# Splitting memory pools so that the next stage's first steps may be issued among the last steps of the stage before

## The chip, the cores and the metric

The kernel runs on one core of one Trainium2 chip. The metric is the device time of one execution in microseconds (us), median of several runs. All numbers of the trace come from one profiled execution of the kernel before.

## The reference, cut to what matters

One layer of a hybrid encoder over a prompt of 2048 frames with 16 meta tokens in front, and over 64 further frames of a running stream. All is in float32.

```python
h = rms_norm(x, attn_norm); z = h @ w_in          # one projection, its columns split into
q_lat, kv_lat, k_rope, qkv, gate, beta, a = split(z)
# group A: latent attention, 8 heads, chunk-causal (chunks of 64 frames)
q = rope(rms_norm(rms_norm(q_lat) @ w_uq)); k = rope(rms_norm([kv_lat @ w_uk, k_rope])); v = kv_lat @ w_uv
attn = softmax(mask(q @ k.T * 96**-0.5)) @ v
# group B: gated delta rule, 4 heads of 128, after a causal convolution of width 4 and SiLU
q, k, v = l2(silu(conv(qkv)));  S_t = decay_t * S_(t-1) + beta_t * k_t (v_t - k_t S)   # in exact chunked form
gdn = rms_norm(q_t S_t) * silu(gate)
x = x + [rms_norm(attn), gdn] @ w_out;  y = x + relu(rms_norm(x) @ w_up)**2 @ w_down
```

The chunked form of the delta rule needs, for each chunk of frames and each head, the inverse of a triangular matrix (independent of other chunks), and then one step of a recurrence in the state S (each chunk after the one before).

## The kernel before

A float32 product is made of three matmuls: each operand is split into a high part and the rest (`split`: a copy on ScalarE and a subtraction on VectorE), and high x high, high x low, low x high are summed in PSUM. [...]

**The program's order.** The kernel is written with pools of named tiles. A pool lies on one of two stacks (left and right), and a tile waits for the users of earlier tiles on its own bytes or its own bank. A scheduler puts the instructions of each engine in one fixed order when the program is built: of the instructions that it holds to be ready it takes the one with the best rank, and the rank is the place in the program. `high_priority(n)` lets the instructions traced inside it rank n places earlier.

**Phase A (`phase_a`), the projection.** The 2128 frames form five blocks (`BLOCKS`: 336, 512, 512, 512 and 256 frames). `load_x` keeps each block's input, split, as `hhi`, `hlo`, all five in one pool `h` (136 KB a partition). The 22 columns of weights (128 wide each) are walked in the order of `BATCHES`; for each batch the blocks are walked, and for each block and column `col_product` makes one product of 24 matmuls (L270 to L272) into a bank `ps` (six banks of the pool `aps`; two more, `psn`, hold sums of squares). `col_finish` multiplies it by `rstd` on VectorE (L282), which frees the bank. Columns 18, 19 and 20, the last, are three of the four columns of the output gate; each is a batch of its own, so the blocks are walked three times. Their SiLU takes three steps on ScalarE (L369 to L371) and one on VectorE (L372), and goes to `gateT` in memory. `load_w` brings a column's weights through two buffers `wraw` (L256), scales them on VectorE (L258) and splits them (L134, L135).

**Phase G (`phase_g`), the delta rule.** It goes by rounds. In each round every open generator takes one step: the preparations of chunks (`gdn_prep`, at most `GK` = 4 at once, a new one when the round and the counts `GR`, `GF`, `GL0`, `GA` allow it), the recurrence of one chunk (`gdn_scan`), and, from round `QS` on, `q_gen` (the queries, 17 tiles, in a pool on the right stack) and after it the attention's first keys and the first part of `prep` of its first job. A preparation loads `kv` and `kq` (L446, L448), turns k (L455), makes squares, an inverse root (`rsqrt`: two steps on ScalarE, L141 and L142, four on GpSimd, L143 to L146) and the normalised keys `kn` (L485, VectorE), turns these (L489), and goes on to the triangular inverse, in banks `gpp` (5 banks). A scan makes the new values (L598, L599), the new state `S` (L605, L607) and the output `o` (L619, L627), squares it, makes an inverse root over ScalarE and GpSimd, scales `o` on GpSimd (L638) and turns it (L642), in banks `gps` (2 banks). All tiles lie in one pool `g`, all seven banks in one pool.

**Attention (`attention`).** 32 jobs (a pair of heads, one of the two, a block of 512 queries). `prep` of a job turns the queries into `qh`, `ql` (L935), makes the scores' row maxima in banks `pspre` (L964 matmul, L965 maximum on VectorE), turns them (L970) and writes their negative into a row of `qh` by a transfer (L972, L973). `main_block` makes the scores `pss` (L994 to L996), the exponent `P` (L998), its split, and the sum over the values `pso` (L1011 to L1013). Both stand in one pool of PSUM banks, `b_ps`; some tags of SBUF tiles have a part of their buffers in a pool that opens early (`EARLY`), during phase G.

Of the kernel before, what the change touches and what calls it, by code (L numbers as in the profile page):

```python
# [40 lines left out]
RUNS = [(0, 1), (1, NS), (NS, NS + 1), (NS + 1, 18)]  # L41
BATCHES = [[21, 3, 4]] + [[5 + i] for i in range(12)] + [[17], [0, 1, 2], [18], [19], [20]]
WRB, APB, ZTB, XTB = 2, 6, 6, 4
# [3 lines left out]
GB = {"kq": 4, "qk": 5, "kd": 5, "vn": 5, "uf": 5, "wt": 5, "ss": 5, "kv": 2, "sq": 1, "kn": 1, "lg": 1, "dm": 2, "db": 1, "bn": 1,  # L47
      "kneg": 3, "bh": 4, "bl": 4, "tt": 5, "uu": 5, "q16": 2, "rk": 3, "se": 1, "vw": 2, "S": 3, "o1": 1, "o": 1, "fr": 2}
GR, GK, GA, GF, GL0 = 6, 4, 5, 2, 4
QSB, QS = 2, 5  # L50
EARLY = {"lath0": 1, "latl0": 1, "kr0": 1, "ssr0": 1, "V0": 2, "KTh0": 2, "KTl0": 2, "raw": 1, "rt": 1,
         "wkv_h": 1, "wkv_l": 1, "qn": 1, "qh": 1, "ql": 1, "kn": 1, "ksq": 2, "kss": 2, "krk": 2, "ktmp": 2}
QP = 2
# [65 lines left out]
class Prog:  # L119
# [42 lines left out]
    def phase_a(self):  # L162
        nc, I = self.nc, self.I
        with ExitStack() as es:
# [21 lines left out]
            for n, batch in enumerate(BATCHES):  # L186
                nxt = BATCHES[n + 1] if n + 1 < len(BATCHES) else []
                Wn = [self.load_w(ct) for ct in nxt[:3 - len(batch)]]
                for b in range(len(BLOCKS)):
                    zs = []  # L190
                    for ct, w in zip(batch, W):
                        ps = self.col_product(w, b)
# [19 lines left out]
    def load_x(self, b):  # L212
# [3 lines left out]
        n = b1 - b0  # L216
        hi = self.hp.tile([128, 8, n], F32R, name=f"hhi{b}")
        lo = self.hp.tile([128, 8, n], F32R, name=f"hlo{b}")
        self.h.append((hi, lo))
# [17 lines left out]
    def mean_rstd(self, ss, n, w, r=None):  # L237

        nc = self.nc
        ps = self.aps.tile([128, NB], F32, name="ps_n", tag="psn", bufs=2)  # L240
        nc.tensor.matmul(ps[:, :n], self.ones, ss, start=True, stop=True)
# [19 lines left out]

    def col_product(self, w, b):

# [168 lines left out]
    def gt(self, tag, bufs=1, shape=(128, 4, 128), dt=F32):  # L432
        return self.gp.tile(list(shape), dt, name=tag, tag=tag, bufs=GB.get(tag, 1))

    def gpsum(self, kind="p"):
        return self.gps.tile([128, 4, 128], F32, name="gp" + kind, tag="gp" + kind, bufs=GPS[kind])

# [210 lines left out]
    def phase_g(self, g=True, q=True, eb=None):  # L648

        with ExitStack() as es:  # L650
            eq = es.enter_context(ExitStack())
            qp = self.pool(eq, "q", side="right")
            qps = self.pool(eq, "q_ps", space=PSUM, side="right")
            self.gp = self.pool(es, "g")
            self.gps = self.pool(es, "gps", space=PSUM)
            self.state = None
            self.lev = [[self.gp.tile([128, 4, 128], F16, name=f"lev{j}{i}") for i in range(7)] for j in range(NL)]
            qg = self.q_gen(qp, qps) if q else iter(())
            ek = None
            for _ in range(QP):  # L660
                next(qg, None)
            Ps = [{"first": i < NL} for i in range(len(CHUNKS))]
            preps, scan, started, scanned, rounds = [], None, 0, 0, 0
            began = [-GL0] * NL
            while g and scanned < len(CHUNKS):

                if rounds >= max((started - GF) * GR, began[started % NL] + GL0) and len(preps) < GK and started < min(len(CHUNKS), scanned + GA):
                    preps.append(self.gdn_prep(CHUNKS[started], Ps[started]))
                    began[started % NL] = rounds
                    started += 1  # L670
                rounds += 1
                if rounds > QS:
                    if ek is not None:
                        if next(ek, "x") == "x" and self.first_prep is None:
                            self.first_prep = self.prep((0, 0, 0))
                            next(self.first_prep)
                    elif next(qg, "x") == "x" and eb is not None:
                        eq.close()
                        self.attn_early(eb)
                        ek = self.early_keys = self.keys(0, 0)  # L680
                if scan is None and "uf" in Ps[scanned]:
                    scan = self.gdn_scan(CHUNKS[scanned], Ps[scanned])
                if scan is not None and next(scan, "x") == "x":
                    scan, scanned = None, scanned + 1
                for p in list(preps):
                    if next(p, "x") == "x":
                        preps.remove(p)
            for _ in qg:
                pass
# [107 lines left out]
    def bpsum(self, tag):  # L797
        k = self.count.get("ps" + tag, 0)
        self.count["ps" + tag] = k + 1
        early = tag == "m" and (self.bp is None or k % BPS["m"] == 0)  # L800
        pool, n = (self.eps_, 1) if early else (self.bps, BPS[tag] - (tag == "m"))
        return pool.tile([128, 512], F32, name="ps" + tag, tag=tag, bufs=n)
# [231 lines left out]
    def attention(self):  # L1034
        with ExitStack() as es:
# [57 lines left out]

            while prep and prep[0][2] == 0:
                prep_step()
            for n, job in enumerate(jobs):
# [834 lines left out]
```

## Time and profile before

| | us |
|---|---|
| median of 3 runs (lowest, highest) | 3327.87 (3316.88, 3330.03) |
| the profiled execution | 3322.66 |
| its span | 3320.9 |
| TensorE busy | 3196.8 (96%) |
| VectorE busy | 2650.8 (80%) |
| ScalarE busy | 1558.4 (47%) |
| GpSimd busy | 400.5 (12%) |

The span is the time from the first to the last instruction of the profile. PE is TensorE's matmuls, DVE VectorE, ACT ScalarE, POOL GpSimd, SP SyncE, whose queue issues most transfers. PEclk is the clock that was granted to TensorE, as a share of full speed. Busy times of one engine do not overlap, those of different engines do.

### The profile page before, as it was taken

How to read it: one execution, taken by the hardware profiler on the slowest of the kernel's cores; microseconds unless marked ns; L12 is line 12 of the kernel's file. 1: busy time of each engine (PE TensorE's matmuls, PEld its weight loads, DVE VectorE, ACT ScalarE, POOL GpSimd, SP SyncE). 2: the span in 40 equal slices, each digit the busy share in tenths (PEclk: the TensorE clock that was granted, in tenths of full speed). 3: DMA queues.
4: the chain of work that ended last, by engine and by line, in shares of the span. 5: the costliest groups of instructions: out<-in, count | busy, mean ns of one | idle time of the engine just before them, and what ended most of it. 6: DMA issues, size and time to landing. Idle time of an engine off the chain costs nothing.

```text
span 3320.9 us, 54512 instructions
## 1 busy us (share of the span) xinstructions
PE 3196.8 (96%) x20037; PEld 2943.1 (89%) x20037; DVE 2650.8 (80%) x5438; ACT 1558.4 (47%) x3495; POOL 400.5 (12%) x758
## 2 busy tenths in 40 slices
PE   9999998998979999999899999999999999999999
PEld 6888887888867778887799999999999999999999
DVE  8877654788758788888789888888888888988887
ACT  5555524555536868787564222334333333422232
POOL 0100013675510000000201000011000002100000
PEclk9999998999978999999999999999999999999999
DMA  4322213233221011010332222233222225122222
GB/s 132 91 74 70 74 63 100 87 104 100 59 57 35 20 34 34 25 37 26 106 99 75 77 77 75 76 110 109 88 76 73 65 73 160 58 73 77 77 74 70
DMA packets 318091, 248.09 MB, mean 75 GB/s; under 512 B 31776, under 2 KB 291616, under 8 KB 317760
## 3 DMA queue, kind: packets, MB, share of 16 engines
q1 hardware_dynamic: 300256, 219.21, 22.8%
q10 hardware_dynamic: 15536, 16.23, 1.6%
q0 software_dynamic: 2032, 9.18, 0.8%
q8 instruction: 157, 2.57, 0.3%
q14 instruction: 110, 0.90, 0.1%
HBM read 196.99 MB, written 47.52 MB: 74 GB/s over the span
## 4 chain that ended last, share of the span: by engine, by line
PE 83%; DVE 8%; ACT 2%; DMA 2%; issue 2%; POOL 1%; SPq 0%; POOLq 0%; DVEq 0%; ACTq 0%
PE psu L1601 23%; PE psd L1601 21%; PE ps L270 5%; PE ps L271 5%; PE ps L272 5%; PE pss L994 2%; PE pso L1011 2%; PE pss L995 2%; PE pss L996 2%; PE pso L1013 2%; PE pso L1012 2%; PE pspre L964 2%; DVE hl L1581 0%; PE psm L889 0%; DMA qh<-mrow 0%
## 5 line engine op out<-in xcount | busy, mean ns | idle before, releaser
L1601 PE MATMUL psu<-hh,uh 128*128 128x352 f32 x1728 | 563.0, 326 | 2.6 <-ACT uh L1497 2.1
L1601 PE MATMUL psu<-hl,uh 128*128 128x352 f32 x1728 | 557.3, 323 | 0.0
L1601 PE MATMUL psu<-hh,ul 128*128 128x352 f32 x1728 | 549.9, 323 | 0.0
L1601 PE MATMUL psd<-al,dh 128*128 128x352 f32 x1536 | 496.0, 323 | 3.5 <-DVE al L1790 3.2
L1601 PE MATMUL psd<-ah,dl 128*128 128x352 f32 x1536 | 494.6, 322 | 0.0
L1601 PE MATMUL psd<-ah,dh 128*128 128x352 f32 x1536 | 473.3, 324 | 11.1 <-DVE y L1709 7.4
L1709 DVE TENSOR_TENSOR y<-y,psd 128x352 f32<-128x352 f32 x768 | 386.6, 515 | 103.5 <-PE psd L1601 101.5
L1601 PEld LDWEIGHTS psu<-hh,uh 128*128 128x128 f32 x1728 | 325.7, 189 | 4.5 <-ACT uh L1497 2.5
L1601 PEld LDWEIGHTS psu<-hl,uh 128*128 128x128 f32 x1728 | 326.1, 189 | 1.2 <-issue 0.5
L1601 PEld LDWEIGHTS psu<-hh,ul 128*128 128x128 f32 x1728 | 323.9, 188 | 0.2 <-DVE ul L1475 0.2
L270 PE MATMUL ps<-hhi,whi 128*128 128x512 f32 (+5 forms) x880 | 313.6, 360 | 9.7 <-ACT hhi L134 7.1
L272 PE MATMUL ps<-hhi,wlo 128*128 128x512 f32 (+5 forms) x880 | 314.0, 358 | 0.0
L271 PE MATMUL ps<-hlo,whi 128*128 128x512 f32 (+5 forms) x880 | 312.5, 356 | 0.3 <-DVE hlo L135 0.2
L1601 PEld LDWEIGHTS psd<-ah,dh 128*128 128x128 f32 x1536 | 284.1, 188 | 16.9 <-DVE y L1709 11.5
L1601 PEld LDWEIGHTS psd<-al,dh 128*128 128x128 f32 x1536 | 289.1, 188 | 5.5 <-DVE al L1790 5.4
L1497 ACT CAST dh<-wr 128x512 fp32r<-128x512 f32 x192 | 119.3, 621 | 367.2 <-PE psd L1601 324.8
L1601 PEld LDWEIGHTS psd<-ah,dl 128*128 128x128 f32 x1536 | 288.8, 188 | 0.0
L1788 ACT CAST ah<-u 128x352 fp32r<-128x352 f32 x192 | 93.4, 487 | 398.6 <-DVE u L1786 280.0
L135 DVE TENSOR_TENSOR Pl<-P,Ph 128x512 fp32r<-128x512 f32 (+4 forms) x352 | 211.2, 611 | 52.2 <-ACT Ph L134 49.7
L998 ACT ACTIVATE P<-pss 128x512 f32<-128x512 f32 (+4 forms) x352 | 185.9, 539 | 87.6 <-PE pss L996 76.9
L965 DVE TENSOR_REDUCE mp<-pspre 128x1 f32<-128x296 f32 (+6 forms) x400 | 189.1, 500 | 31.1 <-PE pspre L964 29.2
L1714 POOL TENSOR_TENSOR y<-y,v 128x352 f32<-128x352 f32 x40 | 40.8, 1043 | 1330.8 <-DVE y L1709 1330.7
(458 smaller groups left out, 7266.5 us busy)
## 6 DMA issues: line engine op xcount, KB each, us to landing
wr<-in_w_up SPq DMA_DIRECT2D x192, 256.0 KB
wr<-in_w_down SPq DMA_DIRECT2D x192, 256.0 KB
qn<-scr_qN SPq DMA_DIRECT2D x32, 384.0 KB
wr<-in_w_out SPq DMA_DIRECT2D x48, 256.0 KB
wraw<-in_w_in SPq DMA_DIRECT2D x42, 256.0 KB
scr_convT<-s SPq DMA_DIRECT2D x36, 256.0 KB
mixr<-scr_mixT SPq DMA_DIRECT2D x12, 704.0 KB
out_y_T<-y SPq DMA_DIRECT2D x48, 176.0 KB
```

The source lines that it names most:

```text
L135: (lo_eng or nc.vector).tensor_tensor(lo, src, hi.bitcast(F32), op=ALU.subtract)
L270: nc.tensor.matmul(ps[:m, :n], whi[:, k, :m], hi[:, k], start=k == 0, stop=False)
L271: nc.tensor.matmul(ps[:m, :n], whi[:, k, :m], lo[:, k], start=False, stop=False)
L272: nc.tensor.matmul(ps[:m, :n], wlo[:, k, :m], hi[:, k], start=False, stop=k == 7)
L964: nc.tensor.matmul(ps[:, :z - a], qh[:r, i * 128:(i + 1) * 128], kh[:r, a:z], start=True, stop=True)
L965: nc.vector.tensor_reduce(m[:, i:i + 1] if one else mp[:, j:j + 1], ps[:, :z - a], axis=AX.X, op=ALU.max)
L994: nc.tensor.matmul(ps[:w, off:], kh[:r, s:s + w], qh[:r, off:], start=True, stop=False)
L998: nc.scalar.activation(p[:w, off:], ps[:w, off:], AF.Exp)
L1497: self.nc.scalar.copy(t[0], src)
L1601: self.nc.tensor.matmul(ps, w, h, start=i == 0, stop=i == len(steps) - 1)
L1709: adds.append(nc.vector.tensor_tensor(Y[j][:, d], Y[j][:, d], ps, op=ALU.add).ins)
L1788: done = nc.scalar.copy(A[f, j][0], u).ins
```

## The change

The projection's columns 18, 19 and 20 become one batch. Each block's `h` gets a pool of its own. The two banks `psn` get a pool of their own on the right side (`apn`); the pool `aps` with the six banks is closed before the last batch, and the last batch's products take the two `psn` banks. In phase G a new pool `g_early` is opened below `g`; of each tag's buffers a part (`EG`) lies there and the rest in `g`, in the same rotation. The banks `p` and `s` get a pool each. The first two steps of the queries and the first `HR` = 12 rounds rank `HO` = 360 places earlier. In the attention, `m`, `mp` and `mrow` get a buffer in the early pool, the banks are divided into two pools (`pre` and `s`, `o` and `m`), and the steps of the first job's `prep` before the first main block rank `AO` = 150 places earlier.

```diff
-BATCHES = [[21, 3, 4]] + [[5 + i] for i in range(12)] + [[17], [0, 1, 2], [18], [19], [20]]
+BATCHES = [[21, 3, 4]] + [[5 + i] for i in range(12)] + [[17], [0, 1, 2], [18, 19, 20]]
...
+EG = {"kv": 2, "kq": 3, "lg": 1, "ss": 3, "sq": 1, "dm": 2, "db": 1, "rk": 3, "vn": 3, "kn": 1, "bn": 1, "qk": 3, "kd": 2, "kneg": 2,
+      "bh": 3, "bl": 3, "tt": 3, "uu": 3, "q16": 1, "uf": 1}
...
+HR, HO = 12, 360
+AO = 150
...
-         "wkv_h": 1, "wkv_l": 1, "qn": 1, "qh": 1, "ql": 1, "kn": 1, "ksq": 2, "kss": 2, "krk": 2, "ktmp": 2}
+         "wkv_h": 1, "wkv_l": 1, "qn": 1, "qh": 1, "ql": 1, "kn": 1, "ksq": 2, "m": 1, "mp": 3, "mrow": 1, "kss": 2, "krk": 2, "ktmp": 2}
...
-            self.hp = self.pool(es, "h")
+            self.hp = [self.pool(es, f"h{b}") for b in range(len(BLOCKS))]
...
-            self.aps = self.pool(es, "aps", space=PSUM)
+            self.apn = self.pool(es, "apn", space=PSUM, side="right")
+            ea = es.enter_context(ExitStack())
+            self.aps = self.pool(ea, "aps", space=PSUM)
...
+                if not nxt:
+                    ea.close()
...
-        ps = self.aps.tile([128, NB], F32, name="ps", tag="ps", bufs=APB)
+        if last:
+            ps = self.apn.tile([128, NB], F32, name="ps", tag="psn", bufs=2)
+        else:
+            ps = self.aps.tile([128, NB], F32, name="ps", tag="ps", bufs=APB)
...
     def gt(self, tag, bufs=1, shape=(128, 4, 128), dt=F32):
-        return self.gp.tile(list(shape), dt, name=tag, tag=tag, bufs=GB.get(tag, 1))
+        k, n, e = self.gcount.get(tag, 0), GB.get(tag, 1), EG.get(tag, 0)
+        self.gcount[tag] = k + 1
+        early = k % n < e
+        return (self.ge if early else self.gp).tile(list(shape), dt, name=tag, tag=tag, bufs=e if early else n - e)
...
+            self.ge, self.gcount = self.pool(es, "g_early"), {}
             self.gp = self.pool(es, "g")
-            self.gps = self.pool(es, "gps", space=PSUM)
+            self.gps = {k: self.pool(es, "gp" + k, space=PSUM) for k in "ps"}
...
-            for _ in range(QP):
-                next(qg, None)
+            with self.tc.high_priority(HO):
+                for _ in range(QP):
+                    next(qg, None)
...
+                with ExitStack() as early:
+                    if rounds < HR:
+                        early.enter_context(self.tc.high_priority(HO))
...
-        self.bps = self.pool(es, "b_ps", space=PSUM)
+
+        a, b = (self.pool(es, "b_ps" + k, space=PSUM) for k in "ab")
+        self.bps = {"pre": a, "s": a, "o": b, "m": b}
...
-            while prep and prep[0][2] == 0:
-                prep_step()
+            with self.tc.high_priority(AO):
+                while prep and prep[0][2] == 0:
+                    prep_step()
```

The body of a round is unchanged inside the new `with`.

## Rows read from the trace of the kernel before

**Rows 1.** The page: busy time and instructions of each engine; granted clock in 40 slices.

```profile
PE 3196.8 (96%) x20037; PEld 2943.1 (89%) x20037; DVE 2650.8 (80%) x5438; ACT 1558.4 (47%) x3495; POOL 400.5 (12%) x758
...
PEclk9999998999978999999999999999999999999999
```

**Rows 2.** Busy time by stretch: length, PE, PEld, DVE, ACT, POOL busy (instructions), clock, DMA.

```profile
540.00:550.00 10.00, 2.05 (x16) 1.59 (x14) 7.28 (x18) 5.13 (x26) 6.41 (x15) 0.82 0.79 247
550.00:560.00 10.00, 9.19 (x45) 8.12 (x45) 6.94 (x13) 4.04 (x8) 6.62 (x6) 0.50 0.43 112
560.00:600.00 40.00, 35.33 (x294) 29.50 (x293) 25.65 (x57) 20.14 (x71) 25.86 (x49) 0.83 0.24 67
600.00:700.00 100.00, 94.95 (x884) 84.07 (x883) 80.09 (x161) 55.18 (x192) 67.04 (x138) 0.98 0.34 98
945.00:985.00 40.00, 28.00 (x107) 22.47 (x108) 23.77 (x72) 15.73 (x46) 5.88 (x16) 0.59 0.26 73
```

**Rows 3.** Timeline of PE around the first seam: start, length, instruction [idle before, releaser].

```profile
468.76 0.32 PE L270 MATMUL ps<-hhi,whi 128*128 128x336 f32 x1
...
515.88 0.32 PE L270 MATMUL ps<-hhi,whi 128*128 128x336 f32 x1
...
519.58 0.40 PE L270 MATMUL ps<-hhi,whi 128*128 128x512 f32 x1
...
538.81 0.60 PE L455 MATMUL gpp<-ident,kv 128*16 128x128 f32 x4
...
550.46 0.57 PE L489 MATMUL gpp<-ident,kn 16*128 16x16 f32 x4 [8.11 <-DVE kn L485]
...
559.91 0.44 PE L728 MATMUL qp<-wuq_h,ql_h 128*128 128x384 f32 x1
```

**Rows 4.** Timeline of SP's queue around the first seam.

```profile
519.62 0.37 SPq L446 DMA_DIRECT2D kv<-scr_convT  x1
...
541.87 0.82 SPq L700 DMA_DIRECT2D qs<-in_w_uq  x2
```

**Rows 5.** Timeline of PE up to the attention's first scores.

```profile
814.46 0.62 PE L935 MATMUL psm<-ident,qn 128*96 128x128 f32 x4
...
936.03 1.12 PE L642 MATMUL gps<-ident,o 128*128 128x128 f32 x4 [5.07 <-POOL o L638]
936.94 0.64 PE L598 MATMUL gps<-vn,uf 128*128 128x128 f32 x2
...
948.87 1.12 PE L642 MATMUL gps<-ident,o 128*128 128x128 f32 x4 [5.12 <-POOL o L638]
949.64 1.12 PE L964 MATMUL pspre<-KTh,qh 105*128 105x144 f32 x3
951.04 0.94 PE L964 MATMUL pspre<-KTh,qh 96*128 96x264 f32 x2 [0.28 <-DVE m L965]
...
958.43 0.58 PE L889 MATMUL psm<-wkv_h,lath 128*128 128x256 f32 x1 [0.41 <-ACT mrow L972]
...
961.15 0.63 PE L994 MATMUL pss<-qh,KTh 97*80 97x512 f32 x1
```

**Rows 6.** Timeline of DVE around the first seam.

```profile
530.70 0.69 DVE L282 TENSOR_TENSOR zt<-ps,rstd 128x512 f32<-128x512 f32 x1 [1.94 <-PE ps L272]
...
536.14 0.69 DVE L282 TENSOR_TENSOR zt<-ps,rstd 128x512 f32<-128x512 f32 x1 [1.94 <-PE ps L272]
539.01 0.42 DVE L282 TENSOR_TENSOR zt<-ps,rstd 128x256 f32<-128x256 f32 x1 [2.18 <-PE ps L272]
...
549.64 0.68 DVE L485 TENSOR_TENSOR kn<-gpp,rk 16x512 f32<-16x512 f32 x1 [2.66 <-POOL rk L146]
```

**Rows 7.** Timeline of DVE: the weights loaded for the last column.

```profile
477.01 1.34 DVE L258 TENSOR_TENSOR wraw<-wraw,g_attn 128x512 f32<-128x512 f32 x2 [2.59 <-DMA wraw<-in_w_in]
...
478.87 0.69 DVE L135 TENSOR_TENSOR wlo<-wraw,whi 128x512 fp32r<-128x512 f32 x1
```

**Rows 8.** Timeline of DVE: the state that the last chunk reads.

```profile
928.32 0.69 DVE L607 TENSOR_TENSOR S<-se,gps 128x512 f32<-128x512 f32 x1 [0.66 <-PE gps L605]
```

More of the change, by code (lines that the diff above doesn't have):

```diff
@@ L191, in phase_a @@
                     for ct, w in zip(batch, W):
-                        ps = self.col_product(w, b)
+                        ps = self.col_product(w, b, n + 1 == len(BATCHES))
                         new = n == 0 and ct == batch[0]
@@ L216, in load_x @@
         n = b1 - b0
-        hi = self.hp.tile([128, 8, n], F32R, name=f"hhi{b}")
-        lo = self.hp.tile([128, 8, n], F32R, name=f"hlo{b}")
+        hi = self.hp[b].tile([128, 8, n], F32R, name=f"hhi{b}")
+        lo = self.hp[b].tile([128, 8, n], F32R, name=f"hlo{b}")
         self.h.append((hi, lo))
@@ L239, in mean_rstd @@
         nc = self.nc
-        ps = self.aps.tile([128, NB], F32, name="ps_n", tag="psn", bufs=2)
+        ps = self.apn.tile([128, NB], F32, name="ps_n", tag="psn", bufs=2)
         nc.tensor.matmul(ps[:, :n], self.ones, ss, start=True, stop=True)
@@ L260, in load_w, with col_product @@
         return hi, lo, m
-    def col_product(self, w, b):
+    def col_product(self, w, b, last=False):
         nc = self.nc
@@ L432, in gt @@
     def gt(self, tag, bufs=1, shape=(128, 4, 128), dt=F32):
-        return self.gp.tile(list(shape), dt, name=tag, tag=tag, bufs=GB.get(tag, 1))
+        k, n, e = self.gcount.get(tag, 0), GB.get(tag, 1), EG.get(tag, 0)
+        self.gcount[tag] = k + 1
+        early = k % n < e
+        return (self.ge if early else self.gp).tile(list(shape), dt, name=tag, tag=tag, bufs=e if early else n - e)
     def gpsum(self, kind="p"):
-        return self.gps.tile([128, 4, 128], F32, name="gp" + kind, tag="gp" + kind, bufs=GPS[kind])
+        return self.gps[kind].tile([128, 4, 128], F32, name="gp" + kind, tag="gp" + kind, bufs=GPS[kind])
     def gdn_prep(self, n, P):
@@ L653, in phase_g @@
             qps = self.pool(eq, "q_ps", space=PSUM, side="right")
+            self.ge, self.gcount = self.pool(es, "g_early"), {}
             self.gp = self.pool(es, "g")
-            self.gps = self.pool(es, "gps", space=PSUM)
+            self.gps = {k: self.pool(es, "gp" + k, space=PSUM) for k in "ps"}
             self.state = None
-            self.lev = [[self.gp.tile([128, 4, 128], F16, name=f"lev{j}{i}") for i in range(7)] for j in range(NL)]
+            self.lev = [[self.ge.tile([128, 4, 128], F16, name=f"lev{j}{i}") for i in range(7)] for j in range(NL)]
             qg = self.q_gen(qp, qps) if q else iter(())
             ek = None
-            for _ in range(QP):
-                next(qg, None)
+            with self.tc.high_priority(HO):
+                for _ in range(QP):
+                    next(qg, None)
             Ps = [{"first": i < NL} for i in range(len(CHUNKS))]
@@ L665, in phase_g @@
             while g and scanned < len(CHUNKS):
[L667 to L687, printed above, removed]
+                with ExitStack() as early:
+                    if rounds < HR:
+                        early.enter_context(self.tc.high_priority(HO))
+                    if rounds >= max((started - GF) * GR, began[started % NL] + GL0) and len(preps) < GK and started < min(len(CHUNKS), scanned + GA):
+                        preps.append(self.gdn_prep(CHUNKS[started], Ps[started]))
+                        began[started % NL] = rounds
+                        started += 1
+                    rounds += 1
+                    if rounds > QS:
+                        if ek is not None:
+                            if next(ek, "x") == "x" and self.first_prep is None:
+                                self.first_prep = self.prep((0, 0, 0))
+                                next(self.first_prep)
+                        elif next(qg, "x") == "x" and eb is not None:
+                            eq.close()
+                            self.attn_early(eb)
+                            ek = self.early_keys = self.keys(0, 0)
+                    if scan is None and "uf" in Ps[scanned]:
+                        scan = self.gdn_scan(CHUNKS[scanned], Ps[scanned])
+                    if scan is not None and next(scan, "x") == "x":
+                        scan, scanned = None, scanned + 1
+                    for p in list(preps):
+                        if next(p, "x") == "x":
+                            preps.remove(p)
@@ L800, in bpsum @@
         early = tag == "m" and (self.bp is None or k % BPS["m"] == 0)
-        pool, n = (self.eps_, 1) if early else (self.bps, BPS[tag] - (tag == "m"))
+        pool, n = (self.eps_, 1) if early else (None if self.bp is None else self.bps[tag], BPS[tag] - (tag == "m"))
         return pool.tile([128, 512], F32, name="ps" + tag, tag=tag, bufs=n)
```

## Prediction

> **What bounds the kernel now.** The page's table of busy times comes first: TensorE (PE) is busy for 3196.8 of 3320.9 us, 96%, so whatever the change may win lies in the 124.1 us in which PE stands, and in the stretches where its clock is granted at half. The line of clocks says where to look: it falls to 8 in the seventh of 40 slices (498 to 581 us), to 7 in the twelfth (913 to 996) and to 8 in the one behind it, and nowhere else [rows 1]. The seventh and the twelfth are the seams that the change touches, from the projection to the delta rule and from there to the attention. The busy times by stretch measure them [rows 2]. [...] Counting busy time times the missing clock as lost, 540 to 600 us loses 13.4 us idle + 9.19 x 0.50 + 35.33 x 0.17 = 24.0 us, and does 36.0 us of work at full clock.
>
> The timeline of PE says what it waited for [rows 3]. The delta rule's first transposes follow the last product at 538.81, and a little later PE waits 8.11 us, until 550.46, for kn, the normalised keys of the first chunk: transposes, squares on ScalarE, an inverse root that goes over VectorE, ScalarE and GpSimd, and back to VectorE. Nothing else is in PE's queue: all products are done, and the query work starts only at 559.91. The start of the delta rule was not held by its loads: the first kv was issued at 519.62, as the last column's product over block 0 ended [rows 4]. It was held by the order: phase A's instructions come earlier in the program and rank higher.
>
> At the other seam the same view shows PE waiting 5.07 and 5.12 us for o of the last two chunks (ScalarE, then GpSimd), then five short waits, 0.28 us first and 0.41 last, 2.85 us together, while the row maxima of the attention's first job are made [rows 5]; the first score matmul comes at 961.15. From 945 to 985 us PE is busy for 28.00 of 40 us at a clock of 0.59 [rows 2].
>
> **The change, part by part.** *Batches and pools of the projection.* Columns 18, 19, 20 become one batch, so the five blocks are walked once, with three products each, instead of three times. The number of matmuls stays. A product over 512 frames takes 5.44 us (evictions at 530.70 and 536.14), one over 256 takes 2.87 (to 539.01) [rows 6]. Once block 2 has its three products, 3 x (5.44 + 2.87) = 24.9 us of products are left; once block 1 has, 41.3 us. With a pool for each block's h, the 85.3 KB of g_early (sum of its tags' sizes) end inside h0, h1 and h2 (87.0 KB), and its first tags, up to vn, inside h0 and h1. The six banks of aps are closed before the last batch, which goes through the two banks of apn: the delta rule's five "p" banks are then free. So the first chunks may run while 25 to 41 us of products remain.
>
> *The boost.* The first 12 rounds (HR) rank 360 instructions earlier. The last batch has 15 products of 24 matmuls and some six other instructions, about 450, so these rounds rank among its blocks 1 to 4. By the start conditions the preps of chunks 0, 1, 2 and 17 fall into them. Their matmuls are not fewer. What goes is the idle time at the seam, with products as cover. I price it by the next stretch, where several preps share PE: 600 to 700 us loses 100 - 94.95 + 94.95 x 0.02 = 6.9 us per 100 [rows 2]. The 36.0 us of work would take 36.0 / 0.931 = 38.7 instead of 60 us: 21.3 us gained. Bounds: 24.0 if every wait is covered, 0 if the same waits return later (rivals).
>
> *What the batch adds.* All three columns' weights pass two raw buffers at the batch's start. In the run of before the batch's first product started at 468.76, and one over block 0's 336 frames takes 3.70 us (515.88 to 519.58) [rows 3], so the third column will be wanted at 476.2. The raw weights that were loaded third there were scaled from 477.01 and had their first low part done at 479.56 [rows 7]: late by 3.4 us, or by 0 if PE is given a product over block 1 meanwhile. I take 3.4. The evictions now share VectorE with the delta rule and have one spare buffer: a kn that waits 2.66 us and takes 0.68 [rows 6] delays an eviction by 3.3 us. The slack is one product less the eviction, 4.75 us at 512 frames, 2.45 at 256: nothing at the former, 0.9 us for each of three products at the latter, 0 to 2.7 us. I take 0, since the wait would have to fall on block 4. [...]
>
> *Queues.* SP carries the kv and kq loads of the four preps among the gateT stores of columns 18 and 19. A store stands in the queue until its y is done, and the loads behind it with it; a load that is late by one product is covered by products. The query work keeps its place: its pool lies over rstd, which the last eviction reads, so its loads come after the projection as now (541.87) [rows 4]. The boost on its first two steps buys nothing.
>
> *The end.* m, mp and mrow move to a pool that is open early, "pre" and "s" get five banks of their own, on those that the last prep frees, and job 0's maxima rank 150 instructions earlier. Their PE work, 1.12 + 0.94 = 2.06 us, fits into the wait of 5.07 us, since the query it reads was turned at 814.46, after its keys [rows 5]. With them the five waits of 2.85 us go: together 4.9 us. Bounds: 0, if the scores are held by something else; 5.07 + 5.12 + 4.9 us, if scores fill both waits, and 28.00 x 0.41 = 11.5 us more if the clock stays up: 26.6. I take 4.9, nearer to the low end, because the two waits are the scan's own latency and remain, and what follows is a chain through ScalarE and VectorE.
>
> Sum: 21.3 - 3.4 + 4.9 = 22.8 us, off the profiled execution's 3322.66 us (its span is 3320.9, 1.8 us lie around it): **3300 us**. The median of the runs shown, 3327.87, lies 5.2 us above that execution, and the runs spread over 3316.88 to 3330.03; I do not shift for it. About 0.5% (16.6 us) is what a measurement of this kernel tells from no change: faster is below 3311.2, slower above 3344.5.
>
> **Rivals.** *Both seams close* (0.12): 24.0 + 26.6 us, 3272 us. For it: the bounds above. Against it: the scan's waits.
>
> *The loss is moved* (0.28). When the products run out the query work is still 18.0 us from its first matmul (541.87 to 559.91), so PE again has preps alone and the stretch from 540 to 560, which lost 7.95 idle + 0.81 idle + 4.6 clock = 13.4 us, and the waits behind it come back, some 25 us later. Gain 0 to 6.5 at the start, 0 to 4.9 at the end: 3311 to 3323 us. Against it: by then four preps are under way, where before there were two with the same wait.
>
> *Waits stand before products* (slower, 0.10). The order in PE's queue is fixed when the program is built. If the builder takes the chain to kn for shorter than it is, the transposes of kn stand ahead of ready products and PE waits with work behind it. This happened at the end: the matmuls of the last chunk's v (936.94) stood behind the transposes of o for 5.07 us, though the state S that they read was written at 929.01 [rows 5, 8]. A chain costs 8.11 us and 4.6 us at half clock, 12.7 us. There are four in the boosted rounds: 50.8 us for the 24.0 of today, 3349 us, 3345 with the gain at the end. At two it is even; with the fourth it is slower by over 0.5%. Against it: from 600 to 700 us, with the same chains, PE loses only 5.05 us idle. [...]
>
> **Numbers.** Forecast 0.50 (3287 to 3311), both seams 0.12, moved 0.28, slower 0.10. Faster by over 0.5% is the first two, 0.62; within 0.5% the third, 0.28; slower 0.10. The range runs from 3272, the bound of gain, to 3332: no gain at either seam, the weights' 3.4 us and the evictions' 2.7 (3328.8), and 3 us for the spread of the runs; about 0.85 of the chance lies inside.
>
> **What would show it.** Right: matmuls with gpp between products, the wait for kn of 8 us gone, no stretch at 0.50 after the projection, pspre matmuls before the transposes of the last o, and the first score some 5 us nearer to the last chunk's end. Wrong: products that wait for ps or whi, idle PE with DVE kn as releaser among products, a new low clock when the products end, or the first score still behind the transfer of mrow.

## The result and the profile after

The changed kernel is slower: 3351.31 us (median of 5, 3340.38 to 3351.96) against 3321.56 us of the kernel before in the same runs, a ratio of 1.0074 [1.0052, 1.0096]. The forecast was 3300 us and "faster". The profiled execution took 3340.38 us (span 3338.7), the quickest of the five at a mean granted clock of 0.976; the three at 3351 us show 0.971.

The page of the changed kernel, busy times and granted clock:

```profile
PE 3205.8 (96%) x20037; PEld 2951.2 (88%) x20037; DVE 2642.8 (79%) x5438; ACT 1553.1 (47%) x3495; POOL 399.0 (12%) x758
...
PEclk9999998999878999999899999999999999999999
```

The same number of matmuls is done. The clock line has two dips more than before [rows 1]: the eleventh slice (835 to 918 us) and the twentieth (1586 to 1669). Busy times by stretch, changed kernel, in the columns of [rows 2]:

```profile
460.00:500.00 40.00, 34.05 (x194) 30.69 (x194) 27.12 (x47) 15.50 (x30) 3.52 (x2) 0.91 0.27 95
...
540.00:550.00 10.00, 10.00 (x71) 8.49 (x71) 3.21 (x9) 4.55 (x15) 3.63 (x5) 1.00 0.29 79
550.00:560.00 10.00, 9.14 (x81) 8.68 (x81) 7.59 (x14) 5.24 (x15) 6.59 (x11) 1.00 0.33 87
560.00:600.00 40.00, 37.20 (x339) 28.90 (x339) 25.11 (x64) 20.37 (x70) 20.03 (x30) 0.74 0.33 98
600.00:700.00 100.00, 93.02 (x892) 83.60 (x890) 77.02 (x158) 54.09 (x194) 66.17 (x140) 1.00 0.34 99
700.00:900.00 200.00, 172.15 (x1761) 160.47 (x1761) 149.55 (x324) 95.65 (x351) 108.60 (x209) 0.92 0.32 88
945.00:985.00 40.00, 24.67 (x142) 21.38 (x142) 21.04 (x58) 15.53 (x52) 7.90 (x17) 0.77 0.23 66
```

and two of these stretches in the kernel before:

```profile
460.00:500.00 40.00, 40.00 (x236) 35.94 (x235) 29.26 (x51) 18.88 (x35) 3.53 (x2) 1.00 0.30 103
```

```profile
700.00:900.00 200.00, 180.48 (x1983) 165.84 (x1982) 160.56 (x352) 107.97 (x393) 117.30 (x217) 0.97 0.33 87
```

Counting lost time as the prediction does (idle, and busy time times the missing clock): the first seam, 540 to 600 us, loses 0.86 + 2.80 + 37.20 x 0.26 = 13.3 us, 10.7 less than the 24.0 of before (the prediction left out 2.05 x 0.18 = 0.4 us of clock from 540 to 550 us). But 460 to 500 us, which lost nothing, now loses 5.95 + 34.05 x 0.09 = 9.0 us; and 700 to 900 us, a stretch to which the prediction gave no term, loses 27.85 + 172.15 x 0.08 = 41.6 us where it lost 19.52 + 180.48 x 0.03 = 24.9: 16.7 us. From 600 to 700 us nothing changed, 7.0 against 6.9. The same stretches of time hold other work in the two kernels (1761 matmuls and 1983 in the last one), so the sums say where time is lost and not yet what was slowed; the turns of o below do that.

Timeline of PE in the changed kernel: the start of the batch of three, and the first seam.

```profile
476.36 0.32 PE L284 MATMUL ps<-hhi,wlo 128*128 128x336 f32 x1
482.23 0.62 PE L282 MATMUL ps<-hhi,whi 128*128 128x336 f32 x1 [5.56 <-DVE zt L294]
...
526.49 0.60 PE L470 MATMUL gpp<-ident,kv 128*16 128x128 f32 x4
...
538.36 0.42 PE L504 MATMUL gpp<-ident,kn 16*128 16x16 f32 x4
...
558.61 0.28 PE L284 MATMUL ps<-hhi,wlo 128*128 128x256 f32 x1
...
571.73 0.67 PE L749 MATMUL qp<-wuq_h,ql_h 128*128 128x384 f32 x1
```

The delta rule starts 12.3 us earlier (526.49, before 538.81), its transposes of kn come among products without a wait, and the last product is at 558.61. The query work, which stayed behind the projection, moved with it: its first matmul is at 571.73 in place of 559.91 [rows 3]. The wait of 5.56 us at 482.23 is the new one. VectorE's timeline around it:

```profile
477.44 1.28 DVE L140 TENSOR_TENSOR wlo<-wraw,whi 128x512 fp32r<-128x512 f32 x2
478.65 2.07 DVE L337 SCALAR_TENSOR_TENSOR zt<-zt,g_qa,nr 128x512 f32<-128x512 f32 x3
...
481.57 0.51 DVE L294 TENSOR_TENSOR zt<-ps,rstd 128x336 f32<-128x336 f32 x1 [0.52 <-DMA scr_qlatT<-zt]
482.25 0.51 DVE L294 TENSOR_TENSOR zt<-ps,rstd 128x336 f32<-128x336 f32 x1 [0.17 <-DMA scr_qlatT<-zt]
```

PE ends the first two products at 476.7 and the third column's weights are ready at 478.7. What PE waits for last is one of its two banks: the evictions that free them stand behind the norms of columns 0 to 2 (L337), and then for a `zt` buffer that a store of the query latents still reads.

Timeline of PE at the other end of the delta rule, and the first wait of that kind behind the attention, changed kernel:

```profile
948.22 0.68 PE L987 MATMUL pspre<-KTh,qh 105*128 105x144 f32 x3
...
953.79 1.11 PE L657 MATMUL gps<-ident,o 128*128 128x128 f32 x4 [3.62 <-POOL o L653]
...
966.62 1.12 PE L657 MATMUL gps<-ident,o 128*128 128x128 f32 x4 [5.12 <-POOL o L653]
...
971.11 0.71 PE L1017 MATMUL pss<-qh,KTh 97*80 97x512 f32 x1 [2.15 <-DMA qh<-mrow]
...
1616.85 0.79 PE L1224 MATMUL psk<-wuk_h,lat_l 128*128 128x512 f32 x1 [2.48 <-DVE gq L1207]
```

The row maxima begin before the last two turns of o. From the last turn to the first score it is 4.5 us, where it was 961.15 - 948.87 = 12.3 [rows 5], 7.8 us less. These two stretches, before and changed:

```profile
948.87:961.15 12.28, 9.43 (x34) 7.57 (x35) 8.37 (x26) 3.28 (x8) 1.85 (x5) 0.50 0.22 69
```

```profile
966.62:971.11 4.49, 1.50 (x6) 0.80 (x6) 3.33 (x12) 1.76 (x5) 0.51 (x3) 0.50 0.18 59
```

Only half of the 7.8 us is lost time: 2.85 + 9.43 x 0.50 = 7.57 us before and 2.99 + 1.50 x 0.50 = 3.74 now, 3.8 less. The other half is work that was moved: products of the keys (`psm<-wkv`) which stood ahead of the first score now come behind it.

But the turns themselves, which begin 22.5 us ahead of before (632.45 and 654.97 us), end 17.7 us behind it. Part of that lead was no gain: the query work was put off, its last matmul is at 765.07 in place of 739.42. From the 3rd turn of the main sequence to the 7th it takes 110.6 us in place of 86.8, and from the 7th to the 12th 103.8 in place of 85.9. The first of these, before and changed:

```profile
725.02:811.77 86.75, 75.06 (x800) 69.14 (x799) 71.35 (x161) 45.22 (x167) 48.33 (x93) 0.92 0.38 99
```

```profile
696.35:806.95 110.60, 93.71 (x912) 87.09 (x913) 88.02 (x183) 55.70 (x200) 70.36 (x143) 0.94 0.38 107
```

There 112 matmuls more are done, and the lost time is 22.5 us against 17.7. From the 7th to the 12th it is 21.5 against 6.6: that stretch, shown below, is where most of the time is lost.

Behind the attention PE waits 2.48 us for gq, which the kernel before doesn't; that one waits 2.1 us in all (1.41 and 0.69) for `sq` in the same part. From the last score to the end it is 1733.9 us against 1727.9. So of the 17.8 us by which the two profiled spans differ, the first score has 10.0, the attention adds 1.8 and what follows it 6.0; where these 6.0 arise is open.

### The profile page after: what moved, and what is told of

It reads as the page before. It is cut to its first block, busy times and chain, and to the rows that moved or that the text cites. A ratio compares the mean times of both kernels' runs of the same rounds, so it can differ in the third digit from the quotient of the medians.

```text
span 3338.7 us, 54536 instructions
## 1 busy us (share of the span) xinstructions
PE 3205.8 (96%) x20037; PEld 2951.2 (88%) x20037; DVE 2642.8 (79%) x5438; ACT 1553.1 (47%) x3495; POOL 399.0 (12%) x758
## 3 DMA queue, kind: packets, MB, share of 16 engines
q1 hardware_dynamic: 300256, 219.21, 22.5%
## 4 chain that ended last, share of the span: by engine, by line
PE 46%; DVE 4%; issue 1%; DMA 0%; ACT 0%; POOL 0%; POOLq 0%; DVEq 0%; ACTq 0%; SPq 0%
PE psu L1625 23%; PE psd L1625 21%; DVE hl L1605 1%; DMA mixr<-scr_mixT 0%; DVE al L1814 0%; DVE t L1805 0%; DVE y L1733 0%; PE psk L1224 0%; PE psk L1222 0%; DVE u L1810 0%; PE psk L1223 0%; PE psk L1281 0%; PE psk L1282 0%; PE psk L1280 0%; DVE hl L1761 0%
## 5 line engine op out<-in xcount | busy, mean ns | idle before, releaser
L1625 PE MATMUL psd<-ah,dh 128*128 128x352 f32 x1536 | 473.7, 324 | 11.2 <-DVE y L1733 7.4
L1733 DVE TENSOR_TENSOR y<-y,psd 128x352 f32<-128x352 f32 x768 | 386.2, 514 | 102.5 <-PE psd L1625 100.7
L282 PEld LDWEIGHTS ps<-hhi,whi 128*128 128x128 f32 (+1 forms) x880 | 164.4, 187 | 42.3 <-issue 7.6
```

The lines of the kernel that those rows point to most:

```text
L282: nc.tensor.matmul(ps[:m, :n], whi[:, k, :m], hi[:, k], start=k == 0, stop=False)
L1625: self.nc.tensor.matmul(ps, w, h, start=i == 0, stop=i == len(steps) - 1)
L1733: adds.append(nc.vector.tensor_tensor(Y[j][:, d], Y[j][:, d], ps, op=ALU.add).ins)
```

## The experiments

All ratios are to the kernel before, run on the same chip in the same rounds. "7 to 12" is the time from the transposes of the 7th chunk's o to those of the 12th, where the queries are done and only keys and chunks are left; "first score" is the attention's first score matmul; both from the one profiled execution. Executions of one kernel differ: gl3_noend took 3323.64 us at a mean granted clock of 0.982 and 3347.02 at 0.974, with one order of instructions. The profiled one is the quickest of its kernel in changed, batchonly, perm and swap_gf1, and the slowest in startonly, endonly, swap_gl3, gl3_noend and before_gl3, so the last two columns say where time lies in one execution and do not add up to the ratios. Numbers of lines are those of the changed kernel.

| kernel | ratio | 7 to 12, us | first score, us |
|---|---|---|---|
| before | 1 | 85.9 | 961.2 |
| changed | 1.0074 [1.0052, 1.0096] | 103.8 | 971.1 |
| single: three single batches | 1.0016 [1.0008, 1.0025] | 86.2 | 949.2 |
| noboost | 1.0109 [1.0096, 1.0122] | 107.3 | 984.3 |
| startonly: attention as before | 1.0073 [1.0060, 1.0086] | 100.9 | 985.0 |
| endonly: before with the end part | 1.0016 [1.0006, 1.0025] | 86.5 | 966.2 |
| batchonly: before with a batch of three | 1.0054 [1.0040, 1.0067] | 92.3 | 969.1 |
| single_start: single, attention as before | 1.0018 [1.0009, 1.0026] | 85.6 | 957.6 |
| perm: batch 20, 18, 19 | 1.0059 [1.0045, 1.0073] | 99.4 | 965.8 |
| swap17: 0 to 2 ahead of 17 | 1.0023 [1.0012, 1.0035] | 103.9 | 954.2 |
| single_hr8: single, HR = 8 | 1.0095 [1.0078, 1.0111] | 111.6 | 976.0 |
| swap_gf3: swap17, GF = 3 | 1.0028 [1.0017, 1.0038] | 98.2 | 961.1 |
| swap_gl3: swap17, GL0 = 3, HR = 20 | 0.9997 [0.9987, 1.0007] | 100.3 | 956.5 |
| swap_gf1: swap17, GF = 1, HR = 20 | 1.0026 [1.0013, 1.0038] | 93.6 | 958.4 |
| gl3_noend: swap_gl3, attention as before | 1.0040 [1.0024, 1.0056] | 97.8 | 960.6 |
| gl3_onebps: swap_gl3, one pool of banks | 1.0011 [0.9998, 1.0024] | 103.7 | 965.7 |
| before_gl3: before with GL0 = 3 | 1.0109 [1.0096, 1.0122] | 102.5 | 979.3 |

**The parts of the change, undone or alone.** The theory then was that the batch on two banks costs 8 us, and the boost puts the delta rule ahead of the query work that fills its waits.

```diff
 # single
-... [17], [0, 1, 2], [18, 19, 20]]
+... [17], [0, 1, 2], [18], [19], [20]]
 # noboost
-HR, HO = 12, 360
+HR, HO = 0, 360
-            with self.tc.high_priority(HO):
-                for _ in range(QP):
-                    next(qg, None)
+            for _ in range(QP):
+                next(qg, None)
 # startonly (and, the other way round, endonly)
-"m": 1, "mp": 3, "mrow": 1,
...
-        a, b = (self.pool(es, "b_ps" + k, space=PSUM) for k in "ab")
-        self.bps = {"pre": a, "s": a, "o": b, "m": b}
+        self.bps = self.pool(es, "b_ps", space=PSUM)
...
-            with self.tc.high_priority(AO):
-                while prep and prep[0][2] == 0:
-                    prep_step()
+            while prep and prep[0][2] == 0:
+                prep_step()
```

> The changed kernel with columns 18, 19 and 20 as three batches again (everything else as changed; only the last of them uses the two banks). Theory A: the batch of three starts with two banks where it had six, and PE loses some 8 us at 460 to 500 us, since VectorE is late with the evictions there; with single batches that stretch loses under 2 us, and the time is 3340 to 3345, while the rest of the loss (the delta rule between 650 and 900 us, some 16 us) stays. Rival B: the batch costs nothing that comes through to the end; then 3351 as the changed kernel.

> The changed kernel without the priorities of phase G (HR = 0, and none on the first two steps of the queries); pools, batch and end as changed. Theory A: the boosted rounds put the delta rule ahead of the query work that fills its waits later; without them the seam waits again as before (9 us from 540 to 560), the 8 us at 480 stay, 650 to 900 us loses some 26 us as before and not 41, and the end keeps its 8 us: 3320 to 3333. Rival C: it is the divided pools and banks that cost, not the order; then 650 to 900 us loses about 40 us here too and the time is 3345 to 3360.

> The changed kernel with the attention as before (EARLY without m, mp and mrow, one pool of banks, no AO): the start part alone. Theory A: the end part gains some 8 us between the last chunk and the first scores, so this one is slower than the changed kernel, 3355 to 3362, with the row maxima behind the last transposes of o again. Rival D: the end part gives its gain back later or costs by itself; then 3335 to 3350.

> The kernel before with the end part alone (m, mp and mrow early, banks pre and s apart from o and m, AO = 150). Theory A: the first scores come some 8 us after the last transposes of o less than before, and the rest follows: 3312 to 3317. Rival D: what is gained is lost again at the next seam, where the last layer's first products wait: 3320 to 3330.

The theory failed in all four. Single batches took off 23 us, not 7: 3328.05 us, outside what either theory gave. Without the boost the kernel is not quicker but slower, 3358.05 us, inside the range of rival C, the divided pools; but single has these pools too, and takes 3328.05, so the pools by themselves are not what costs. The end part by itself costs 6 us on the kernel before (3328.16) and gains nothing on the start part (3347.10 without it); both times are inside rival D's ranges. But endonly does not test the mechanism, since the maxima did not move there:

```profile
955.07 1.11 PE L643 MATMUL gps<-ident,o 128*128 128x128 f32 x4 [5.11 <-POOL o L639]
955.84 1.12 PE L966 MATMUL pspre<-KTh,qh 105*128 105x144 f32 x3
```

They stand behind the last turn of o as before, and from that turn to the first score it is 11.2 us against 12.3. What single showed beside the stall is in the third column: its chunks 7 to 12 take 86 us like those of before, while the three others of the changed kernel's family (changed, noboost, startonly), with a batch of three, take 101 to 107.

**The batch by itself.**

```diff
 # batchonly, on the kernel before; perm and swap17, on the changed kernel
-[17], [0, 1, 2], [18], [19], [20]]
+[17], [0, 1, 2], [18, 19, 20]]
-[17], [0, 1, 2], [18, 19, 20]]
+[17], [0, 1, 2], [20, 18, 19]]
-[17], [0, 1, 2], [18, 19, 20]]
+[0, 1, 2], [17], [18, 19, 20]]
```

> The kernel before with columns 18, 19 and 20 as one batch and nothing else changed: six banks, one pool, no priorities. Theory A (the batch of three costs because two banks cannot cover VectorE's lateness at 480 us): no loss at 460 to 500 us, since the six banks cover it, and 3320 to 3327. Rival E (the batch of three itself leads to another order of the delta rule, with 20 us a chunk between the 8th and the 12th in place of 17): no loss at 480 us but some 16 us lost from 750 to 900, and 3332 to 3345.

> The start part alone with three single batches (attention as before). If the parts add, the end part's 4 to 6 us go off the 3328 of the kernel with single batches: 3320 to 3324, no gain over the kernel before though the first seam loses some 8 us less. If the start part by itself gains what it gains at its seam: 3308 to 3316.

> The changed kernel with its last batch in the order 20, 18, 19: the same work, the same banks, another order of three columns. Theory E (a batch of three on two banks costs by its place): the loss at 480 and the slower chunks stay, 3345 to 3355. Rival F (the slower chunks are an accident of the order in which the builder happens to put the delta rule, which any small change may turn): the 480 us stall stays, the chunks may go back to 17 us, and the time may be anything from 3325 to 3355.

> The changed kernel with columns 0, 1, 2 ahead of column 17, so that their norms and stores are done when the batch of three starts. Theory: the stall at 480 us comes from VectorE's work on columns 0 to 2 meeting two banks; it goes, 6 to 8 us, and the chunks stay slow: 3340 to 3345. If the stall stays, it is the batch's own evictions or weights: 3350.

The stretch from 460 to 500 us, batchonly and then swap17:

```profile
460.00:500.00 40.00, 40.00 (x225) 35.82 (x224) 29.06 (x50) 18.39 (x35) 4.14 (x3) 1.00 0.31 102
```

```profile
460.00:500.00 40.00, 40.00 (x212) 35.53 (x211) 18.16 (x35) 20.12 (x37) 0.28 (x1) 1.00 0.23 84
```

The stall is settled by both: with six banks it is covered though VectorE does much the same work (29.06 us busy against 27.12), and with columns 0 to 2 a batch earlier VectorE is busy for 18.16 us in place of 27.12 and the two banks do. That swap17 gains 20 us and not the 9 of the stall is not fully traced. From the 3rd turn of the main sequence to the 7th it takes 90.7 us (699.99 to 790.67), the changed kernel 110.6 (696.35 to 806.95), but with 104 matmuls fewer there; of these 19.9 us, 7.4 are lost time:

```profile
699.99:790.67 90.68, 78.73 (x808) 72.89 (x807) 74.08 (x162) 47.37 (x176) 56.39 (x116) 0.96 0.39 112
```

batchonly takes 1.0054 of the time of before with no stall at all, inside the range of rival E, that the batch itself leads to another order; but its profiled execution, the quickest, loses 9.5 us more than before from 750 to 900 us, not 16. perm, at 3345.27 us, is inside the ranges of both its theories and decides nothing. single_start, 3329.18 us, missed both of its ranges and is level with single: without the batch of three the start part gains nothing either.

**The order of the later chunks.** All kernels so far trace the delta rule in the same program order; what differs is the order in which the builder put the instructions of the engines. (Those below with another GF or GL0 start preparations in other rounds, so their program order differs too.) The built orders of before and of batchonly have the same sequence of operations on PE from the first turn of o to that of the fifth chunk, and part there, where the attention's first keys come in. In the traces PE's sequence of operations from the 7th turn to the 12th is one and the same in before, single, single_start and endonly, which take 85.6 to 86.5 us; in the thirteen others it is another one, and they take 92.3 to 111.6. If it is this order that costs, then a kernel with single batches must become slow too when something small turns it:

```diff
 # single_hr8, on single
-HR, HO = 12, 360
+HR, HO = 8, 360
```

> The kernel with three single batches (3328, o's turns of chunk 7 to 12 86 us apart) with 8 boosted rounds in place of 12, so that the builder arrives at another order of the later chunks: the one that the changed kernel has, with the transposes of kn ahead of the new chunk's first products. Theory F (the order of the later chunks is what costs, and small things turn it): chunks 7 to 12 take 100 to 107 us and the time is 3340 to 3350, with no batch of three. Rival E (the batch of three costs): 3326 to 3332.

3353.72 us: 26 us for four boosted rounds less, with three single batches. Theory F held in kind; time and chunks are somewhat above its ranges. Both kernels have the 7th chunk's turn at nearly the same time (802.82 and 804.87). Chunks 7 to 12 in the kernel before, the changed kernel, single and single_hr8:

```profile
811.77:897.68 85.91, 79.31 (x930) 72.60 (x929) 66.00 (x143) 46.35 (x172) 49.04 (x85) 1.00 0.28 71
```

```profile
806.95:910.73 103.78, 90.42 (x976) 84.39 (x973) 71.45 (x163) 48.80 (x188) 48.47 (x86) 0.91 0.23 59
```

```profile
804.87:891.06 86.19, 79.34 (x929) 72.60 (x929) 65.90 (x143) 46.16 (x172) 48.94 (x85) 1.00 0.28 71
...
839.27:857.21 17.94, 15.72 (x185) 14.25 (x184) 13.34 (x30) 9.09 (x34) 9.99 (x17) 1.00 0.29 74
```

```profile
802.82:914.39 111.57, 94.29 (x928) 88.58 (x924) 67.14 (x144) 44.65 (x173) 48.76 (x86) 0.82 0.21 55
...
846.43:869.84 23.41, 19.40 (x189) 18.29 (x186) 13.23 (x29) 8.77 (x35) 9.88 (x18) 0.79 0.22 57
```

928 and 929 matmuls, 25.4 us apart: 17.3 us idle against 6.9, and 94.29 x 0.18 = 17.0 us of clock against none. In the changed kernel it is 13.4 us idle and 8.1 of clock, with 46 matmuls more than before. The second lines are one chunk each: 17.94 us with PE idle for 2.22 at the full clock, 23.41 us with 4.01 idle and 4.07 lost to the clock. The idle time, by PE's waits over the length of one chunk in single_hr8:

```profile
837.59 0.28 PE L561 MATMUL gpp<-lev,lev 128*128 128x64 f16 x4 [1.33 <-DVE uf L589]
...
844.68 1.09 PE L504 MATMUL gpp<-ident,kn 128*128 128x128 f32 x4 [1.32 <-DVE fr L649]
...
847.32 0.64 PE L613 MATMUL gps<-vn,uf 128*128 128x128 f32 x2
...
853.63 1.16 PE L620 MATMUL gps<-vw,kd 128*128 128x128 f32 x8 [0.87 <-DVE vw L616]
```

Three waits of 0.87 to 1.33 us in every full chunk (and one of 0.43), each for a VectorE result, with other chunks' matmuls behind in PE's queue. After the first of them the matmuls come to take 1.6 to 1.9 times as long as in single, until about 849 us (eight of L497 take 1.84 us here and 0.95 in single, two of L613 0.64 us here and 0.39 at 839.71 us in single; the granted clock is 0.77 from 840 to 860 us); behind the wait of 0.87 they don't (L620 takes 1.16 us in both kernels). In single's chunk the longest waits are one of 1.54 and one of 0.49 us, and the clock stays full. In single_hr8 the matmuls behind each of the three waits start after it: L489 on kv at 838.14 us, L561 at 845.56, L634 at 854.62.

**Back to the order of before, and GL0 alone.**

```diff
 # on swap17: swap_gf3; swap_gl3; swap_gf1
-GR, GK, GA, GF, GL0 = 6, 4, 5, 2, 4
+GR, GK, GA, GF, GL0 = 6, 4, 5, 3, 4
+GR, GK, GA, GF, GL0 = 6, 4, 5, 2, 3     # with HR = 20
+GR, GK, GA, GF, GL0 = 6, 4, 5, 1, 4     # with HR = 20
 # on swap_gl3: gl3_noend as startonly above; gl3_onebps only the pools of banks
 # on the kernel before: before_gl3
+GR, GK, GA, GF, GL0 = 6, 4, 5, 2, 3
```

> Columns 0 to 2 ahead of 17, a batch of three, all of the change, and GF = 3 (one more preparation may start early): the builder arrives at the order that the kernel before has for the later chunks. Theory F: no stall at 480 us, chunks 7 to 12 in 86 to 90 us in place of 104, and 3310 to 3318, faster than the kernel before. Rival E: chunks as slow as in the other kernels with a batch of three, 3330.

> As the one before, with 20 boosted rounds, GL0 = 3 and GF = 2: another way to the order of the kernel before for the later chunks. Theory F: 86 to 90 us from chunk 7 to 12, and 3308 to 3318. Rival E: 3330.

> As the one before, with 20 boosted rounds, GF = 1 and GL0 = 4: preparations start later, so the query work fills more of the first chunks; the later chunks in the order of the kernel before. Theory F: 86 us from chunk 7 to 12, and 3308 to 3320. Rival E: 3330.

> The kernel with columns 0 to 2 ahead of 17, a batch of three, 20 boosted rounds and GL0 = 3 (3323, level with the kernel before), now with the attention as before, without the end part. The order of the delta rule stays the same. Theory G (the end part takes at the seam behind the attention what it gives ahead of it): 3316 to 3322. Theory H (the end part gains its 5 to 8 us and the attention's own order costs): 3328 to 3332.

> The same kernel with the end part's buffers and AO = 150, but one pool of banks in the attention. Theory: the row maxima then wait for banks that the last preparation frees, and stand behind the last turns of o again; the wait for gq of some 2.5 us behind the attention, which every kernel with two pools shows, goes. 3320 to 3328: no difference that can be told from 3323.

> The kernel before with GL0 = 3 and nothing else: the builder arrives at another order of the later chunks, one that stands between the two others. Theory F: chunks 7 to 12 take 90 to 100 us in place of 86 and the time is 3328 to 3340, since nothing else changes. If GL0 = 3 is itself a gain: 3310 to 3318.

The first three missed their numbers: 98, 100 and 94 us from chunk 7 to 12, not 86, and none of these chunks has PE's sequence of before, so the way back was not found; swap_gf3 and swap_gf1, at 3332.77 and 3333.98 us, lie near the 3330 of rival E. The best, swap_gl3, is level with the kernel before (3323.32 against 3323.88 us). There the end part does pay: without it 3333.83 us, with one pool of banks 3327.18, which cannot be told from 3323. So it gains 10 us on this kernel, and cost 6 on the kernel before, where the maxima did not move. Theory H had 3328 to 3332. In the traces the stretch from the last turn to the first score is 4.5 us with it and 11.8 without; with one pool of banks it is 11.2, the maxima behind the last turn as expected, but the wait for gq, which was to go, is there (2.47 us). Why the 10 us come to that is open. The three have the same sequence on PE from the 7th turn to the 12th and take 100.3, 97.8 and 103.7 us for it: that is what executions differ by in such an order.

before_gl3 is the plainest of all: one start condition, no pool, no batch, no priority, and 3360.32 us, 37 us more, beyond the 3328 to 3340 that were expected. Its chunks 7 to 12 have much the same matmuls, 933 (before 930):

```profile
809.32:911.81 102.49, 89.28 (x933) 84.14 (x932) 65.27 (x143) 44.43 (x173) 48.53 (x85) 0.87 0.23 60
```

That is 16.6 us of it. The attention behind takes longer as well, with PE as busy as before but at a lower clock; from 1040 to 1600 us, the kernel before, gl3_noend, before_gl3:

```profile
1040.00:1600.00 560.00, 545.35 (x2858) 443.17 (x2858) 459.93 (x1099) 438.59 (x964) 11.28 (x24) 0.98 0.11 30
```

```profile
1040.00:1600.00 560.00, 545.07 (x2789) 438.86 (x2788) 450.79 (x1080) 425.15 (x936) 9.87 (x24) 0.96 0.10 29
```

```profile
1040.00:1600.00 560.00, 541.83 (x2780) 436.42 (x2779) 456.40 (x1100) 421.25 (x933) 10.57 (x25) 0.96 0.10 28
```

2 hundredths of the clock are 545 x 0.02 = 11 us here. From the first score to the last one it is 631.8 us in the kernel before, 652.2 in gl3_noend and 647.7 in before_gl3. The profiled execution of gl3_noend is the slowest of twelve that spread over 23 us, so its 652.2 may be that execution and not its order.

## Why the prediction was wrong, by its own steps

**The start, +21.3: right in kind, half in size.** The chain to kn is covered by products and 540 to 560 us has 0.86 us idle. It brought 10.7 us, because from 560 to 600 us the clock is 0.74. When the products end, PE has preparations alone until 571.73; the clock falls in that stretch and is at 0.50 through the first query matmuls:

```profile
558.90:571.73 12.83, 11.27 (x117) 8.26 (x115) 9.40 (x24) 7.51 (x28) 9.73 (x14) 0.83 0.64 192
571.73:585.00 13.27, 12.03 (x96) 9.46 (x94) 7.81 (x21) 5.34 (x14) 4.16 (x3) 0.50 0.21 61
```

The step "the query work keeps its place ... loads come after the projection as now (541.87)" failed: they come after the projection, but this now ends 20 us later, since PE did the boosted rounds in between; the loads are issued at 562.95. That is what the rival "the loss is moved" said, for about half of the loss.

**What the batch adds, -3.4: the wrong term and too small.** The weights were late by 2.0 us (478.7 against 476.7) and not 3.4, and that lies inside the wait for the bank. The evictions, costed at 0 with a bound of 2.7 us for block 4, cost the 9.0 us, at block 0: I looked for what the delta rule would put in VectorE's way at the end of the batch, and not for what columns 0 to 2 still put there at its start. The same lateness stands in the trace of before, where six banks cover it; batchonly shows that they do, and swap17 that moving the work away does as well.

**The end, +4.9: 7.8 us between the last turn of o and the first score, 3.8 of them lost time.** The maxima went ahead of the turns as forecast. But three of the five waits that were priced at 2.85 us (0.59, 0.78 and 0.79) are for the keys' `kr` and `latl` and not for the maxima; they went because these products moved behind the first score, and the score now waits 2.15 us for the transfer of `mrow`. The new wait of 2.48 us for gq behind the attention stands against 2.1 us for `sq` before. The part did not pay everywhere: +10 us on one kernel, -6 on another, where its maxima did not move.

**The signs.** Of those named for being wrong three came: PE waits for a bank among the products (5.56 us), a new low clock when the products end (0.50 from 571.73 to 585 us), and the first score behind the transfer of mrow (2.15 us). No sign looked between the seams.

**The step that failed** is one that the prediction took without a term: that what lies between the two seams stays as it is. It priced the edits where they are made and took the sum off the whole. In the changed kernel 700 to 900 us lose 16.7 us more than before, and chunks 7 to 12 take 103.8 us in place of 85.9; with the stall of 9.0 us that outweighs the 10.7 us and what the end gives. The builder puts each engine's instructions in order by ranks and its own estimate of times, so a shift of the first chunks can turn the order of the later ones, and the order of the kernel before, with 17 us a chunk at the full clock, turned out to be hard to meet again by the changes that were tried. The rival "waits stand before products" had this mechanism, an order fixed when the program is built, with transposes of kn ahead of ready work, but looked for it among the products, where it did not happen, and priced it at 3349 us by four waits of 8.11 us; that this lies near the measured 3351 is chance. It happens at chunks 7 to 12, with waits of about 1 us in each, and most of the price is the clock (17.0 of 27.4 us in single_hr8, 8.1 of the 14.9 us that the changed kernel loses more).

Shown: the stall at 480 us and its cause (batchonly, swap17); that the order alone costs 26 us with batches, pools and end part held equal (single_hr8 against single), and a changed start condition 37 us without any of them (before_gl3); that in these two the chunks' loss is idle time and clock at equal matmuls. Argued only: that the clock follows from those waits. Adding matmuls to fill them would itself change the order, so it wasn't tried. Open: which of the two, chunks before the 7th or attention, makes up the rest in each kernel (chunks 7 to 12 alone don't: swap_gl3 takes 100.3 us there and is level with before, single_start 85.6 and is 1.0018), the 6.0 us behind the attention of the changed kernel, and an order that has both the early start and 17 us a chunk; none of the kernels beats the one before.

## What to carry to other kernels

Where a builder orders the engines, a change at one seam can be a change to the order of all that follows: before trusting a sum over the edits, ask what the time is worth of the order that exists, and measure it by a change that does nothing else (one start condition, some rounds of priority). Compare the orders of the later stages on each engine first, then the seams. And a buffer count that is cut for the sake of the next stage has to be held against the worst lateness of the stage before, not only against what the change adds.

## What the runs showed of the hardware

In single, PE was busy for 79.34 of the 86.19 us of chunks 7 to 12 and was granted the full clock, a wait of 1.54 us among them. In single_hr8, with the same work cut by three waits of about 1 us a chunk, it was busy for 94.29 of 111.57 us and was granted 0.82. In chunks 7 to 12 of single_hr8 these waits came with 10.4 us more of idle time than in single, and with 17.0 us of clock. And one built kernel is not one time: the twelve executions of gl3_noend spread over 23 us, at mean granted clocks of 0.973 to 0.982.
